# Differential attention in three steps per head, its factor on GpSimd, queries transposed two heads ahead

## The chip, the cores and the metric

The kernel runs on one core of a Trainium2 chip. A core has five engines with a queue each that is worked off in order: TensorE (PE in the profile, its weight loads as PEld), VectorE (DVE), ScalarE (ACT), GpSimd (POOL) and SyncE (SP), which issues DMAs. [...] The metric is the device time of one execution in microseconds (us), the median of several runs.

## The reference, cut to what matters

One transformer block on 512 tokens of width 1024, in fp32: two attention groups side by side on one projection, their joint output projection, a convolutional feed-forward net and a gated embedding. The change lies in the attention.

```
y_mla  = mla_group(...)                       # 8 heads, latent queries and keys
y_diff = diff_group(...)                      # 4 differential heads
x = x + concat([y_mla, y_diff]) @ w_out
x = x + conv_ffn(rms_norm(x), w_gate, w_up, conv_w, conv_b, w_down)
x = x + sigmoid(rms_norm(x) @ w_ple_gate) * (p @ w_ple_proj)

# diff_group, per head and block of queries: two maps m of 64 channels each
logits = einsum('bhqmd,bhmkd->bhmqk', qb, k_t) * scale + bias     # masked
probs  = softmax(logits)
attn   = probs[:, :, 0] - lam * probs[:, :, 1]
o      = rms_norm(attn @ v) * (1 - lam_init)
```

## The kernel before, in words

Every product in fp32 is made of three matmuls on a high and a low part (`mm3`, lines 157 to 159): high by high, low by high, high by low. Splitting a tile into the two parts takes an operation on ACT (high) and one on DVE (low).

The stages, by the span of the profiled execution: projections up to some 70 us; the latent heads (MLA), in 4 pairs by 4 tiles of 128 queries, from 70 to 151; the differential heads from 151 to 218; the rest of the output projection to 238; the feed-forward net to 600; the gated embedding to the end.

The differential stage runs 16 slots, 4 heads by 4 query tiles `t`, tile `t` seeing `(t + 1) * 128` keys. A slot `i` issues, in this order: the logits of slot `i + 2` (`diff_logits`: for each of the two maps the matmuls `dl` into a PSUM bank of the ring `lg`, of 3 banks; on DVE one pass that adds the bias strip and takes the maximum, L733, with a read of its accumulator; on ACT the exponential `pmd`, L734, which also sums the row into `s0` or `s1`); the combination of the two maps of slot `i + 2` (`diff_comb`: reciprocal of `s1` L742, factor `cf` L743, `pm0 + cf * pm1` L744, all on DVE); some units of filling work for PE (`pump`; a unit is six matmuls of 512 columns of the output projection, `o`, and every so often an addition to `x` on DVE, L682); the transposes `pTd` of slot `i`'s probabilities and their copy to SBUF on ACT; and the products `do` with the values for slot `i - 1`. Every head ends with a norm (`sqo`, `sso`, `mo`, `ro` as a power on GpSimd, `yd`) and the transposes `yT` of its output. `diff_T` transposes a head's queries (`d0T`) or keys (`d1T`) into the parts `st`. `FILL_DIFF` says how many units each slot takes; the 20 units come from the first four row blocks of `w_out` (16) and the next four (4). The high parts of the weights are cast on ACT (`hi_o`), the low ones are made on DVE (`lo_o`).

`probs_T` transposes and copies out at once; `mla_T` calls it for the latent heads. The order in which an engine meets its instructions is fixed when the program is built: it follows the order in which the code issues them, with some exchanged by the scheduler. The pool of `pm` tiles has 4 buffers, the PSUM ring `tp` of the transposes 2.

Of the kernel before, what the change touches and what calls it, by code (L numbers as in the profile page):

```python
# [59 lines left out]
FILL_UQ = (1, 1, 1, 1)  # L60
FILL_QK = 5
FILL_MLA = ((2, 2, 2, 2), (2, 2, 2, 2), (2, 2, 2, 2), (1, 1, 1, 1))
FILL_DIFF = ((2, 1, 1, 1), (1, 1, 2, 1), (1, 2, 2, 1), (1, 1, 2, 2))

UP_BANKS = ("lg", "tp", "tp", "ob")

# [28 lines left out]
def hybrid_block(ctx: ExitStack, tc: tile.TileContext, a: dict, out: bass.AP):  # L95
# [444 lines left out]
    pump(FILL_QK)  # L540


    def probs_T(pm, n, name, on_act):

        ps = bank("tp", f"pT{name}")
        for j in range(0, n, P):
            TE.transpose(ps[:, j:j + P], pm[:, j:j + P], ident)
        pt = pt_tile("pt")
        if on_act:
            S.copy(pt[:, :n], ps[:, :n])  # L550
        else:
            V.tensor_copy(pt[:, :n], ps[:, :n])
        return pt
# [62 lines left out]
    def mla_T(hp, t):  # L616

        n = (t + 1) * P
        pm, pmf, sums, one = mla.pop(("pm", hp, t))
        if one:  # L620
            pt = probs_T(pmf, 2 * n, f"m{hp}{t}", t)
            mla["pt", hp, t] = [pt[:, :n], pt[:, n:2 * n]]
        else:
            mla["pt", hp, t] = [probs_T(pm[c], n, f"m{hp}{t}{c}", c) for c in range(2)]

    def mla_pv(hp, t):

# [63 lines left out]
    def wo_units(kq, dqs, nk):  # L691

        for dq in dqs:
            w = wo_w(kq, dq)
            if kq == 0 and dq + 1 in dqs:
                with tc.issue_after(df["comb"].ins):
                    wo_first[0, dq + 1] = wo_w(0, dq + 1)
            if kq:
                wo2[dq] = w
            steps = [(b, k) for b in (2 * dq, 2 * dq + 1) for k in range(0, nk, 2)]  # L700
            if (kq, dq) == (0, 0):
                steps.sort(key=lambda s: s[1])
# [14 lines left out]
        split(h_, l_, ps, dcol if c == 0 else None)  # L717
        df["qk", h, c] = (h_, l_)

    def diff_logits(h, t):  # L720
        n = (t + 1) * P
        if t == 0:
            df["s0", h] = sm.tile([P, NT], F32, tag="s0", name="s0")
        s0 = df["s0", h][:, t:t + 1]
        (qh_, ql_), (kh_, kl_) = df["qk", h, 0], df["qk", h, 1]
        pms, s1 = [], sm.tile([P, 1], F32, tag="s1", bufs=4, name="s1")
        for m in range(2):
            r = slice(64 * m, 64 * m + 64)
            ps = bank("lg", f"dl{h}{t}{m}")
            mm3(ps[:, :n], [(qh_[r, tsl[t]], ql_[r, tsl[t]], kh_[r, :n], kl_[r, :n])])  # L730
            pm = pm_tile("pmd")
            nm = sm.tile([P, 1], F32, tag="nm", bufs=4, name="nmd")
            V.tensor_tensor_reduce(out=pm[:, :n], in0=ps[:, :n], in1=strips[0][:, h, T - n:], scale=1.0, scalar=3e38, op0=ALU.add, op1=ALU.min, accum_out=nm)  # L733
            S.activation(pm[:, :n], pm[:, :n], AF.Exp, bias=nm, scale=-1.0, accum_out=s0 if m == 0 else s1)  # L734
            pms.append(pm)
        df["pm", h, t] = pms, n, s0, s1

    def diff_comb(h, t):

        pms, n, s0, s1 = df["pm", h, t]  # L740
        cf = sm.tile([P, 1], F32, tag="cf", bufs=4, name="cf")
        V.reciprocal(cf, s1)  # L742
        V.scalar_tensor_tensor(cf, cf, nlam, s0, op0=ALU.mult, op1=ALU.mult)  # L743
        df["comb"] = V.scalar_tensor_tensor(pms[0][:, :n], pms[1][:, :n], cf, pms[0][:, :n], op0=ALU.mult, op1=ALU.add)  # L744
        df["pm", h, t] = pms[0]

    def diff_pv(h, t):
        if t == 0:
            df["po"] = bank("ob", f"do{h}")
        po, pt = df["po"], df.pop(("pt", h, t))  # L750
        for j in range(t + 1):
            TE.matmul(po[:, tsl[t]], pt[:, tsl[j]], zd[2][j][:, h * P:(h + 1) * P], start=j == 0, stop=j == t)
        if t < NT - 1:
# [7 lines left out]
        V.reduce_sum(sso, sq.rearrange("p (t d) -> p t d", d=P), axis=AX.X)
# [3 lines left out]
        V.scalar_tensor_tensor(mo, sso, 1.0 / P, mo, op0=ALU.mult, op1=ALU.add)  # L765
        G.tensor_tensor(ro, mo, mhalf[:, :NT], op=ALU.pow)
# [6 lines left out]
    dslots = [(h, t) for h in range(DH) for t in range(NT)]  # L773
    x_sb = []

    def load_x():
# [24 lines left out]
    def first_hi():
        raw = load_raw(a["w_out"][0, 0], 1024, "o00")
        w = [wts.tile([P, 1024], F32R, tag=i, bufs=NW, name=f"{i}_o00") for i in ("hi", "lo")]
        wo_first[0, 0] = w
# [8 lines left out]
        5: [zl(1), sq(0, 3), lambda: zd_root(0)],  # L813
        6: [sq(1, 0), zh(2)],
        7: [zl(2), zh(3)],
        8: [zl(3), sq(1, 1), zs(0, 0), first_hi],
        9: [zl(4), sq(1, 2)],
        10: [sq(1, 3), lambda: zd_root(1), zs(0, 1)],
        11: [zs(0, 2), zs(0, 3)],
        12: [load_x, zs(1, 0), zs(1, 1)],  # L820
        13: [zs(1, 2), zs(1, 3)],
    }
    late = {
        14: [yy(0)],
        15: [yy(1)],
    }
    mla_q(0)
    pump()
# [11 lines left out]
    for hp in range(HP):  # L840
        for t in range(NT):
            i = NT * hp + t
            last = hp == HP - 1
            n = FILL_MLA[hp][t]
            if t:
                mla_norm(hp, t)
            if t < NT - 1:
                mla_logits(hp, t + 1)
            if t == 2:
                for c, (d, m) in enumerate(((diff_T, (0, 0)), (diff_T, (0, 1))) if last else ((mla_q, (2 * hp + 2,)), (mla_k, (2 * hp + 2,)))):  # L850
                    d(*m)
# [717 lines left out]
```

## Time and profile before

| what | value |
|---|---|
| median of 3 runs | 644.52 us (644.42 to 644.86) |
| the profiled execution | 644.82 us, of which its span 643.0 us |
| PE busy | 632.4 us (98%) |
| DVE busy | 486.9 us (76%) |
| ACT busy | 360.2 us (56%) |
| POOL busy | 69.2 us (11%), 94 instructions |
| stage of the differential heads, 151 to 218 us | PE 64.65 of 67.0 us, DVE 56.0, ACT 43.0, POOL 3.0 |

The granted TensorE clock is full throughout. The profile gives the span of one execution on the slowest core; the time has 1.8 us more around it. An engine's busy time is the sum of its instructions' spans, and instructions of an engine overlap a little, so that the distance from one start to the next is what an instruction takes of the queue.

### The profile page before, as it was taken

What the parts mean: (1) busy time and instruction counts of PE and PEld (TensorE: products, weight loads), DVE (VectorE), ACT (ScalarE), POOL (GpSimd) and SP (SyncE); (2) the same over time, 40 slices, a digit from 0 to 9 for tenths busy, and PEclk for the clock granted to TensorE, in tenths of its full rate; (3) what the DMA queues carried; (4) which work ended last, traced back from release to release, by engine and by line L of the source; (5) the groups of instructions that cost most, each with busy time, mean ns of one, the idle gap of its engine ahead of it and who ended that gap; (6) DMA issues with size and microseconds to landing.
All of it is one profiled execution on the core that took longest, in us unless ns stands there. A gap on an engine that the chain in (4) does not pass through costs nothing.

```text
span 643.0 us, 10203 instructions
## 1 busy us (share of the span) xinstructions
PE 632.4 (98%) x3900; PEld 556.2 (87%) x3900; DVE 486.9 (76%) x870; ACT 360.2 (56%) x629; POOL 69.2 (11%) x94
## 2 busy tenths in 40 slices
PE   8999999999999999999999999999999999999997
PEld 8988888876777887889999999999999999988886
DVE  6889667887898678988876767676767777759844
ACT  7896567666667355557555545545454545637111
POOL 1514103030000130001000000000100000000000
PEclk9999999999999999999999999999999999999999
DMA  8241612330221437546865656464646554532021
GB/s 304 100 165 37 182 62 66 99 130 2 66 85 49 164 132 228 148 95 157 208 197 117 184 124 199 117 180 116 180 115 182 118 177 115 181 130 66 27 88 50
DMA packets 29912, 82.63 MB, mean 129 GB/s; under 512 B 3100, under 2 KB 4124, under 8 KB 29736
## 3 DMA queue, kind: packets, MB, share of 16 engines
q1 hardware_dynamic: 23816, 69.17, 32.3%
q0 software_dynamic: 5616, 12.33, 11.3%
q8 instruction: 31, 0.51, 0.3%
q10 hardware_dynamic: 432, 0.49, 0.2%
q14 instruction: 17, 0.14, 0.1%
HBM read 77.77 MB, written 5.52 MB: 130 GB/s over the span
## 4 chain that ended last, share of the span: by engine, by line
PE 86%; DVE 7%; ACT 3%; issue 2%; DMA 1%; ACTq 0%; DVEq 0%; SPq 0%
PE dn L157 6%; PE dn L158 6%; PE dn L159 6%; PE gx L159 4%; PE gx L158 4%; PE gx L157 4%; PE zd L157 3%; PE zd L159 3%; PE zd L158 3%; PE g L157 3%; PE g L158 3%; PE g L159 3%; PE pg L159 2%; PE pg L158 2%; PE pg L157 2%; PE o L157 2%
## 5 line engine op out<-in xcount | busy, mean ns | idle before, releaser
L954 DVE TENSOR_TENSOR wSl<-rS,wSh 128x1024 fp32r<-128x1024 f32 x21 | 25.7, 1224 | 43.4 <-ACT wSh L950 43.2
L157 PE MATMUL dn<-ah,hi_dn 128*128 128x512 f32 x144 | 56.2, 391 | 0.0
L158 PE MATMUL dn<-al,hi_dn 128*128 128x512 f32 x144 | 56.2, 391 | 0.0
L159 PE MATMUL dn<-ah,lo_dn 128*128 128x512 f32 x144 | 56.0, 389 | 0.0
L1071 POOL DMA_DIRECT2D rS<-in_w_gu x19 | 22.7, 1194 | 250.2 <-DVE cv L1239 129.9
L950 ACT CAST wSh<-rS 128x1024 fp32r<-128x1024 f32 x21 | 22.0, 1047 | 35.7 <-PE gy L158 35.4
L157 PE MATMUL zd<-hi_d,xh 128*128 128x512 f32 x96 | 39.1, 407 | 0.0
L158 PE MATMUL zd<-lo_d,xh 128*128 128x512 f32 x96 | 37.6, 392 | 0.0
L682 DVE TENSOR_TENSOR x<-x,dn 128x512 f32<-128x512 f32 x44 | 29.9, 679 | 6.1 <-PE dn L159 6.1
L954 DVE TENSOR_TENSOR wTl<-rA,wTh 128x1024 fp32r<-128x1024 f32 x19 | 23.3, 1225 | 13.7 <-ACT wTh L950 13.2
L159 PEld LDWEIGHTS dn<-ah,lo_dn 128*128 128x128 f32 x144 | 27.0, 188 | 5.8
L157 PEld LDWEIGHTS dn<-ah,hi_dn 128*128 128x128 f32 x144 | 27.1, 188 | 5.1
L158 PEld LDWEIGHTS dn<-al,hi_dn 128*128 128x128 f32 x144 | 27.1, 188 | 5.0
L954 DVE TENSOR_TENSOR wAl<-rA,wAh 128x1024 fp32r<-128x1024 f32 x21 | 25.6, 1217 | 2.7 <-ACT wAh L950 2.7
L950 ACT CAST wAh<-rA 128x1024 fp32r<-128x1024 f32 x21 | 22.1, 1050 | 9.7 <-DMA rA<-in_w_gu 9.5
L1242 ACT ACTIVATE cv<-cv 128x512 f32<-128x512 f32 x22 | 13.9, 630 | 23.9 <-DVE cv L1239 23.8
L157 PE MATMUL g<-b2h,wAh 128*128 128x256 f32 (+1 forms) x88 | 26.4, 300 | 0.5 <-ACT g L1195 0.5
L157 PE MATMUL o<-yh,hi_o 128*128 128x512 f32 x64 | 26.8, 419 | 0.0
L734 ACT ACTIVATE pmd<-pmd,nmd 128x128 f32<-128x128 f32 (+3 forms) x32 | 17.9, 560 | 15.1 <-DVE nmd L733 15.0
L159 PE MATMUL g<-b2h,wAl 128*128 128x256 f32 (+1 forms) x88 | 26.2, 297 | 0.0
L158 PE MATMUL g<-b2l,wAh 128*128 128x256 f32 (+1 forms) x88 | 26.2, 297 | 0.0
L1462 ACT ACTIVATE sg<-sg 128x512 f32<-128x512 f32 (+1 forms) x9 | 5.3, 584 | 36.8 <-DVE sg L1461 36.8
(475 smaller groups left out, 2219.1 us busy)
## 6 DMA issues: line engine op xcount, KB each, us to landing
rA<-in_w_gu SPq DMA_DIRECT2D x22, 512.0 KB, 3.7
rS<-in_w_gu SPq DMA_DIRECT2D x22, 512.0 KB, 3.7
rS<-in_w_gu POOLq DMA_DIRECT2D x19, 512.0 KB, 6.1
raw_dn<-in_w_down SPq DMA_DIRECT2D x18, 512.0 KB, 5.9
raw_d<-in_w_d SPq DMA_DIRECT2D x12, 512.0 KB, 3.4
r<-in_w_gu SPq DMA_DIRECT2D x19, 256.0 KB, 5.9
raw_o<-in_w_out SPq DMA_DIRECT2D x8, 512.0 KB, 3.6
rS_pg<-in_w_pg SPq DMA_DIRECT2D x6, 512.0 KB, 4.1
```

The costliest lines, as they stand in the source:

```text
L157: TE.matmul(ps, xh, wh, start=first and i == 0, stop=False, skip_group_check=again)
L158: TE.matmul(ps, xh, wl, start=False, stop=False, skip_group_check=again)
L159: TE.matmul(ps, xl, wh, start=False, stop=last and i == n - 1, skip_group_check=again)
L682: V.tensor_tensor(xb(b), xb(b), ps, op=ALU.add)
L734: S.activation(pm[:, :n], pm[:, :n], AF.Exp, bias=nm, scale=-1.0, accum_out=s0 if m == 0 else s1)
L950: S.copy(h_, src)
L954: V.tensor_tensor(l_, src, _f32(h_), op=ALU.subtract)
L1071: nc.gpsimd.dma_start(sums[f].rearrange("p (i c) -> p i c", i=2), a["w_gu"][f][:, :2048].rearrange("p (i c) -> p i c", i=2)[:, :, :512], a ...
L1242: S.activation(cv, cv, AF.Silu)
L1462: S.activation(sg, sg, AF.Sigmoid)
```

## The change

Five things are altered together:

- The head's four query tiles are worked in three steps (`GROUPS`): tiles 0 and 2 together, with 128 and 384 keys side by side in one PSUM bank for each map; then tile 1 (256 keys); then tile 3 (512). There are 12 slots in place of 16. The matmuls, maxima, exponentials and combinations are the same in number and size; the copies of transposed probabilities are 12 in place of 16.
- The factor `cf` is computed by three GpSimd instructions of one column each (power -1 against a tile of minus ones, times `nlam`, times `s0`), in place of two on DVE.
- The queries of head `h + 2` are transposed in the middle slot of head `h`; before, those of head `h + 1` in the first slot of head `h`. Head 1's are transposed ahead of the loop.
- `probs_T` is parted: `probs_T` transposes, `probs_out` copies. In the latent heads the last tile of a pair (`t == 3`) issues the maxima and exponentials of the next pair's first tile between the two.
- The units of filling work are dealt out anew, 5 for heads 0 to 2 each and 4 for head 3; two loads of `w_out` are split earlier; the low part of one latent output (`yh1`) is made later.

```diff
-FILL_DIFF = ((2, 1, 1, 1), (1, 1, 2, 1), (1, 2, 2, 1), (1, 1, 2, 2))
+FILL_DIFF = ((2, 1, 2), (2, 1, 2), (2, 1, 2), (1, 1, 2))
...
+    GROUPS = ((0, 2), (1,), (3,))
+    def diff_logits(h, g):
+        ts = GROUPS[g]
...
+        for t in ts:
+            at[t] = slice(n, n + (t + 1) * P)
+            n += (t + 1) * P
+        pms, pss = [], [bank("lg", f"dl{h}{g}{m}") for m in range(2)]
+        for t in ts:
+            for m, ps in enumerate(pss):
+                r = slice(64 * m, 64 * m + 64)
+                mm3(ps[:, at[t]], [(qh_[r, tsl[t]], ql_[r, tsl[t]], kh_[r, :(t + 1) * P], kl_[r, :(t + 1) * P])])
+        for m, ps in enumerate(pss):
             pm = pm_tile("pmd")
-            V.tensor_tensor_reduce(out=pm[:, :n], in0=ps[:, :n], ...)
-            S.activation(pm[:, :n], pm[:, :n], AF.Exp, bias=nm, scale=-1.0, accum_out=s0 if m == 0 else s1)
+            for i, t in enumerate(ts):
+                c = at[t]
+                V.tensor_tensor_reduce(out=pm[:, c], in0=ps[:, c], ...)
+                S.activation(pm[:, c], pm[:, c], AF.Exp, bias=nm, scale=-1.0, accum_out=s0[:, t:t + 1] if m == 0 else s1[:, i:i + 1])
...
-        V.reciprocal(cf, s1)
-        V.scalar_tensor_tensor(cf, cf, nlam, s0, op0=ALU.mult, op1=ALU.mult)
-        df["comb"] = V.scalar_tensor_tensor(pms[0][:, :n], pms[1][:, :n], cf, pms[0][:, :n], op0=ALU.mult, op1=ALU.add)
+        for i, t in enumerate(GROUPS[g]):
+            c, cf = at[t], sm.tile([P, 1], F32, tag="cf", bufs=4, name="cf")
+            G.tensor_tensor(cf, s1[:, i:i + 1], mone, op=ALU.pow)
+            G.tensor_tensor(cf, cf, nlam, op=ALU.mult)
+            G.tensor_tensor(cf, cf, df["s0", h][:, t:t + 1], op=ALU.mult)
+            df["comb"] = V.scalar_tensor_tensor(pms[0][:, c], pms[1][:, c], cf, pms[0][:, c], op0=ALU.mult, op1=ALU.add)
...
             mla_T(hp, t)
-            z_flush()
+            if t < 3:
+                mla_pt(hp, t)
+                z_flush()
             if i:
                 mla_pv(*divmod(i - 1, NT))
-            if t == 3 and not last:
-                mla_logits(hp + 1, 0)
-                for c in range(2):
-                    mla_exp(hp + 1, 0, c)
+            if t == 3:
+                if not last:
+                    mla_logits(hp + 1, 0)
+                    for c in range(2):
+                        mla_exp(hp + 1, 0, c)
+                mla_pt(hp, t)
+                z_flush()
...
-        if h + 1 < DH and t == 0:
-            diff_T(h + 1, 0)
+        if g == 1 and h + 2 < DH:
+            diff_T(h + 2, 0)
-        if t == 3 and h + 2 < DH:
+        if g == 2 and h + 2 < DH:
             diff_T(h + 2, 1)
```

What this does to the queues is seen at three places; `[waits ...]` names the engines on whose semaphores a row waits. First DVE at the end of head 1. `ISA` is the pass over the logits and the read of its accumulator, `SCALAR_TENSOR_TENSOR pmd<-pmd,cf` the combination. Before:

```order
L733 ISA pmd,nmd<-dl_2119,strip 128x512 [waits DVE_49,PE_49]
L733 ISA nmd 128x1
L765 SCALAR_TENSOR_TENSOR mo<-sso,mo 128x4 [waits DVE_49]
L189 SCALAR_TENSOR_TENSOR st<-d0T_2103,dcol,st 128x512 [waits Activation_49]
L682 TENSOR_TENSOR x_1643<-x_1643,o_2077 128x512 [waits PE_49]
L742 RECIPROCAL cf<-s_2110 128x1 [waits Activation_49]
L769 TENSOR_TENSOR yd_2092<-yd_2092,ro 128x512 [waits Pool_49]
L743 SCALAR_TENSOR_TENSOR cf<-cf,nlam,s_1968 128x1 [waits DVE_49]
```

and now:

```order
L756 ISA pmd,nmd<-dl_2082,strip 128x512 [waits PE_49]
L756 ISA nmd 128x1
L795 SCALAR_TENSOR_TENSOR mo<-s_1958 128x4 [waits Activation_49]
L769 SCALAR_TENSOR_TENSOR pmd<-pmd,cf 128x512 [waits Activation_49,Pool_49]
L696 TENSOR_TENSOR x_1645<-x_1645,o_2102 128x512 [waits PE_49]
L792 TENSOR_REDUCE sso<-sqo 128x4 [waits Activation_49]
L796 SCALAR_TENSOR_TENSOR mo<-sso,mo 128x4 [waits DVE_49]
L800 TENSOR_TENSOR yd_2127<-yd_2127,ro 128x512 [waits Activation_49,Pool_49]
L756 ISA pmd,nmd<-dl_2140,strip 128x128 [waits PE_49]
```

The rows between the last pass over the logits and the combination are fewer, the combination waits on GpSimd, `yd` stands right behind the `mo` whose power GpSimd takes, and the next slot's passes stand behind all of it.

The second place is the queue of GpSimd in this stage. Before, it holds the four powers `ro` of the heads' norms:

```order
L165 TENSOR_TENSOR rd<-rs_m,mhalf 128x32 [waits DVE_49] x2
L766 TENSOR_TENSOR ro<-mo,mhalf 128x4 [waits DVE_49] x2
L766 TENSOR_TENSOR ro<-mo,mhalf 128x4 [waits DVE_49,Pool_49] x2
L1007 TENSOR_TENSOR nr_2678<-nr_2678,nsq 128x512 [waits PE_49,Activation_49]
L1007 TENSOR_TENSOR nr_2678<-nr_2678,nsq 128x512 [waits Activation_49,Pool_49] x2
```

and now, at the end of head 1 and the start of head 2, with three rows for each factor:

```order
L766 TENSOR_TENSOR cf<-s_2080,mone 128x1 [waits Activation_49]
L767 TENSOR_TENSOR cf<-cf,nlam 128x1 [waits Pool_49]
L768 TENSOR_TENSOR cf<-cf,s_1958 128x1 [waits Pool_49]
L797 TENSOR_TENSOR ro<-mo,mhalf 128x4 [waits DVE_49]
L766 TENSOR_TENSOR cf<-s_2139,mone 128x1 [waits Activation_49]
L767 TENSOR_TENSOR cf<-cf,nlam 128x1 [waits Pool_49]
L768 TENSOR_TENSOR cf<-cf,s_2138 128x1 [waits Pool_49]
```

Each row of a factor waits for the one before it.

The third is PE ahead of the logits of head 2's tile of 256 keys. Before:

```order
L547 MATMUL pTd_2188<-ident,pmd 128x128 [waits PE_49]
L547 MATMUL pTd_2188<-ident,pmd 128x128 x2
L752 MATMUL do_2143<-zd_1470,pt 128x128 [waits Activation_49]
L752 MATMUL do_2143<-zd_1477,pt 128x128
L665 MATMUL yT_2196<-ident,yd_2092 128x128 [waits DVE_49,PE_49]
L665 MATMUL yT_2196<-ident,yd_2092 128x128 x3
L157 MATMUL dl_2206<-st 128x256
L158 MATMUL dl_2206<-st 128x256
L159 MATMUL dl_2206<-st 128x256
L157 MATMUL dl_2214<-st 128x256 [waits DVE_49]
```

and now:

```order
L783 MATMUL do_2196<-zd_1479,pt 128x128
L783 MATMUL do_2196<-zd_1757,pt 128x128
L729 MATMUL d0T_2201<-ident,zd_791 128x128
L729 MATMUL d0T_2201<-ident,zd_799 128x128
L729 MATMUL d0T_2201<-ident,zd_807 128x128
L729 MATMUL d0T_2201<-ident,zd_815 128x128
L157 MATMUL dl_2210<-st 128x256 [waits DVE_49]
L158 MATMUL dl_2210<-st 128x256
L159 MATMUL dl_2210<-st 128x256
L157 MATMUL dl_2211<-st 128x256 [waits DVE_49]
```

Both banks are now waited for on DVE's semaphore; the bank that `dl_2211` takes is the one that the pass over the 384 logits of the slot before reads.

More of the change, by code (lines that the diff above doesn't have):

```diff
@@ L197, in hybrid_block @@
     V.memset(mhalf, -0.5)
+    mone = small("mone", [P, 1])
+    V.memset(mone, -1.0)
     S.activation(warm[:, :1], ones[:, :1], AF.Exp)
@@ L540, in hybrid_block, with probs_T @@
     pump(FILL_QK)
-    def probs_T(pm, n, name, on_act):
+    def probs_T(pm, n, name):
         ps = bank("tp", f"pT{name}")
@@ L547, in probs_T, with probs_out @@
             TE.transpose(ps[:, j:j + P], pm[:, j:j + P], ident)
+        return ps
+    def probs_out(ps, n, on_act):
         pt = pt_tile("pt")
@@ L620, in mla_T, with mla_pt @@
         if one:
-            pt = probs_T(pmf, 2 * n, f"m{hp}{t}", t)
+            mla["pT", hp, t] = [probs_T(pmf, 2 * n, f"m{hp}{t}")]
+        else:
+            mla["pT", hp, t] = [probs_T(pm[c], n, f"m{hp}{t}{c}") for c in range(2)]
+    def mla_pt(hp, t):
+        n, ps = (t + 1) * P, mla.pop(("pT", hp, t))
+        if t < 2:
+            pt = probs_out(ps[0], 2 * n, t)
             mla["pt", hp, t] = [pt[:, :n], pt[:, n:2 * n]]
         else:
-            mla["pt", hp, t] = [probs_T(pm[c], n, f"m{hp}{t}{c}", c) for c in range(2)]
+            mla["pt", hp, t] = [probs_out(ps[c], n, c) for c in range(2)]
     def mla_pv(hp, t):
@@ L694, in wo_units @@
             w = wo_w(kq, dq)
-            if kq == 0 and dq + 1 in dqs:
+            if kq == 0 and 0 < dq and dq + 1 in dqs:
                 with tc.issue_after(df["comb"].ins):
@@ L718, in diff_T @@
         df["qk", h, c] = (h_, l_)
-    def diff_logits(h, t):
-        n = (t + 1) * P
-        if t == 0:
+    GROUPS = ((0, 2), (1,), (3,))
+    def diff_logits(h, g):
+        ts = GROUPS[g]
+        if g == 0:
             df["s0", h] = sm.tile([P, NT], F32, tag="s0", name="s0")
-        s0 = df["s0", h][:, t:t + 1]
+        s0, s1 = df["s0", h], sm.tile([P, 2], F32, tag="s1", bufs=4, name="s1")
         (qh_, ql_), (kh_, kl_) = df["qk", h, 0], df["qk", h, 1]
[L726 to L730, printed above, removed]
-            pm = pm_tile("pmd")
-            nm = sm.tile([P, 1], F32, tag="nm", bufs=4, name="nmd")
-            V.tensor_tensor_reduce(out=pm[:, :n], in0=ps[:, :n], in1=strips[0][:, h, T - n:], scale=1.0, scalar=3e38, op0=ALU.add, op1=ALU.min, accum_out=nm)
-            S.activation(pm[:, :n], pm[:, :n], AF.Exp, bias=nm, scale=-1.0, accum_out=s0 if m == 0 else s1)
-            pms.append(pm)
-        df["pm", h, t] = pms, n, s0, s1
@@ L738, in diff_comb @@
[L738 to L748, printed above, removed]
-            df["po"] = bank("ob", f"do{h}")
[L750 to L753, printed above, removed]
+        at, n = {}, 0
@@ new lines, in diff_logits @@
+        for t in ts:
[7 more added lines that the diff above has]
+        for m, ps in enumerate(pss):
+            pm = pm_tile("pmd")
+            for i, t in enumerate(ts):
+                c = at[t]
+                nm = sm.tile([P, 1], F32, tag="nm", bufs=4, name="nmd")
+                V.tensor_tensor_reduce(out=pm[:, c], in0=ps[:, c], in1=strips[0][:, h, T - (t + 1) * P:], scale=1.0, scalar=3e38, op0=ALU.add, op1=ALU.min, accum_out=nm)
+                S.activation(pm[:, c], pm[:, c], AF.Exp, bias=nm, scale=-1.0, accum_out=s0[:, t:t + 1] if m == 0 else s1[:, i:i + 1])
+            pms.append(pm)
@@ new lines, in diff_logits, with diff_comb @@
+        df["pm", h, g] = pms, n, at, s1
+    def diff_comb(h, g):
+        pms, n, at, s1 = df["pm", h, g]
+        for i, t in enumerate(GROUPS[g]):
[4 more added lines that the diff above has]
+            df["comb"] = V.scalar_tensor_tensor(pms[0][:, c], pms[1][:, c], cf, pms[0][:, c], op0=ALU.mult, op1=ALU.add)
+        df["pm", h, g] = pms[0], n, at
@@ new lines, in diff_probs, with diff_pv @@
+    def diff_probs(h, g):
+        pm, n, at = df.pop(("pm", h, g))
+        df["pt", h, g] = probs_out(probs_T(pm, n, f"d{h}{g}"), n, True), at
+    def diff_pv(h, g):
+        if g == 0:
+            df["po"] = bank("ob", f"do{h}")
+        po, (pt, at) = df["po"], df.pop(("pt", h, g))
+        for t in GROUPS[g]:
+            for j in range(t + 1):
+                c = at[t].start + j * P
+                TE.matmul(po[:, tsl[t]], pt[:, c:c + P], zd[2][j][:, h * P:(h + 1) * P], start=j == 0, stop=j == t)
+        if g < 2:
@@ L771, in diff_pv @@
             df["scale"] = df["scaling"]()
-    dslots = [(h, t) for h in range(DH) for t in range(NT)]
+    dslots = [(h, g) for h in range(DH) for g in range(3)]
     x_sb = []
@@ L799, in hybrid_block, with first_hi @@
     z2_lo = lambda kq: lo(*z2_[kq])
[L801 to L804, printed above, removed]
+    def first_hi(dq):
+        raw = load_raw(a["w_out"][0, dq], 1024, f"o0{dq}")
+        w = [wts.tile([P, 1024], F32R, tag=i, bufs=NW, name=f"{i}_o0{dq}") for i in ("hi", "lo")]
+        wo_first[0, dq] = w
         z2_.append((*hi(raw, w[0]), w[1]))
@@ L815, in hybrid_block @@
         7: [zl(2), zh(3)],
-        8: [zl(3), sq(1, 1), zs(0, 0), first_hi],
+        8: [zl(3), sq(1, 1), zs(0, 0), lambda: first_hi(0)],
         9: [zl(4), sq(1, 2)],
@@ L819, in hybrid_block @@
         11: [zs(0, 2), zs(0, 3)],
-        12: [load_x, zs(1, 0), zs(1, 1)],
+        12: [load_x, zs(1, 0), zs(1, 1), lambda: first_hi(1)],
         13: [zs(1, 2), zs(1, 3)],
@@ L824, in hybrid_block @@
         14: [yy(0)],
-        15: [yy(1)],
     }
@@ L882, in hybrid_block @@
     mla_pv(HP - 1, NT - 1)
+    y_hl(1, ymn[1])
+    diff_comb(0, 0)
     y_hl(3, mla["po"])
-    diff_comb(0, 0)
     diff_T(1, 1)
     y_hl(2, ymn[2])
+    diff_T(1, 0)
     diff_comb(0, 1)
+    z2_lo(5)
     region.__exit__(None, None, None)
     pump()
-    for i, (h, t) in enumerate(dslots):
+    for i, (h, g) in enumerate(dslots):
         if i + 2 < len(dslots):
@@ L893, in hybrid_block @@
             diff_comb(*dslots[i + 2])
-        pump(FILL_DIFF[h][t])
-        df["pt", h, t] = probs_T(df.pop(("pm", h, t)), (t + 1) * P, f"d{h}{t}", True)
+        pump(FILL_DIFF[h][g])
+        diff_probs(h, g)
         if i:
             diff_pv(*dslots[i - 1])
-        if h + 1 < DH and t == 0:
-            diff_T(h + 1, 0)
-        if h and t == 1:
+        if g == 1 and h + 2 < DH:
+            diff_T(h + 2, 0)
+        if h and g == 1:
             df["scaling"]()
-        if t == 3 and h + 2 < DH:
+        if g == 2 and h + 2 < DH:
             diff_T(h + 2, 1)
-        if h and t == 2:
+        if h and g == 2:
             y_split(4 + h - 1, df["y", h - 1], ocol, "tp")
-        if h and t == 3:
-            if h == 2:
-                fill.append(wo_units(1, range(2), 2))
+        if h == 2 and g == 2:
+            fill.append(wo_units(1, range(2), 2))
     pump()
```

## The prediction

> **What bounds the kernel now.** I read the windows of the differential stage first, then what PE waited for in it, then the groups by line and form for prices, and the timeline for what one start has from the next. The sum of five windows from 151 to 218 us:
>
> ```profile
> sum 67.00, PE 64.65 PEld 51.12 DVE 56.01 ACT 43.03 POOL 3.02; mean PE 12.93 PEld 10.22 DVE 11.20 ACT 8.61 POOL 0.60
> ```
>
> PE has 2.35 us free in 67 and DVE 11, so PE bounds the stage and DVE is not far. PE's waits between 130 and 240 us, longest first:
>
> ```profile
> PE dl L159 <- DVE st L189: 0.9, 2, 0.6
> PE mo L633 <- DVE pt L552: 0.7, 1, 0.7
> PE pTd L547 <- ACT pt L550: 0.5, 1, 0.5
> ```
>
> All that can be gained from waits is 2.1 us. DVE's free time is not spare either, as its timeline around one factor shows:
>
> ```profile
> 176.58 0.17 DVE L742 RECIPROCAL cf<-s 128x1 f32<-128x1 f32 x1 [0.90 <-ACT pmd L734]
> 176.78 0.22 DVE L743 SCALAR_TENSOR_TENSOR cf<-cf,nlam,s 128x1 f32<-128x1 f32 x1
> 177.03 0.62 DVE L744 SCALAR_TENSOR_TENSOR pmd<-pmd,cf 128x384 f32<-128x384 f32 x1
> 177.57 0.68 DVE L733 CUSTOM_DVE_ANT_0 pmd<-dl,strip 128x512 f32<-128x512 f32 x1
> 178.18 0.08 DVE L733 DVE_READ_ACCUMULATOR2_ANT nmd<- 128x1 f32 x1
> 178.18 0.68 DVE L761 TENSOR_REDUCE sso<-sqo 128x4 f32<-128x512 f32 x1
> 178.78 0.68 DVE L733 CUSTOM_DVE_ANT_0 pmd<-dl,strip 128x512 f32<-128x512 f32 x1
> ```
>
> DVE stands 0.90 us for the exponential, then spends 0.45 on the factor; the next pass over logits, which frees a bank for PE, stands behind both. From start to start an instruction takes 0.06 to 0.08 less than its span. The prices, DVE and ACT:
>
> ```profile
> L151 DVE TENSOR_TENSOR lo_o<-raw_o,hi_o 128x1024 fp32r<-128x1024 f32 x7 | 8.5, 1217 | 0.0
> L682 DVE TENSOR_TENSOR x<-x,o 128x512 f32<-128x512 f32 x12 | 8.1, 682 | 0.1
> L733 DVE CUSTOM_DVE_ANT_0 pmd<-dl,strip 128x512 f32<-128x512 f32 x8 | 5.4, 679 | 0.0
> L733 DVE CUSTOM_DVE_ANT_0 pmd<-dl,strip 128x384 f32<-128x384 f32 x8 | 4.3, 550 | 0.3 <-PE dl L159 0.2
> L743 DVE SCALAR_TENSOR_TENSOR cf<-cf,nlam,s 128x1 f32<-128x1 f32 x16 | 3.5, 218 | 0.4
> L733 DVE CUSTOM_DVE_ANT_0 pmd<-dl,strip 128x256 f32<-128x256 f32 x8 | 3.3, 418 | 0.0
> L744 DVE SCALAR_TENSOR_TENSOR pmd<-pmd,cf 128x512 f32<-128x512 f32 x4 | 3.0, 750 | 0.1
> ...
> L742 DVE RECIPROCAL cf<-s 128x1 f32<-128x1 f32 x16 | 2.6, 160 | 3.8 <-ACT pmd L734 3.7
> L744 DVE SCALAR_TENSOR_TENSOR pmd<-pmd,cf 128x384 f32<-128x384 f32 x4 | 2.5, 615 | 0.1
> L189 DVE SCALAR_TENSOR_TENSOR st<-d0T,dcol,st 128x512 fp32r<-128x512 f32 x3 | 2.2, 746 | 0.1
> L733 DVE CUSTOM_DVE_ANT_0 pmd<-dl,strip 128x128 f32<-128x128 f32 x8 | 2.2, 288 | 0.9 <-PE dl L159 0.6
> ```
>
> ```profile
> L734 ACT ACTIVATION_READ_ACCUMULATOR pmd<-pmd,nmd 128x1 f32 x32 | 6.0, 189 | 0.0
> L734 ACT ACTIVATE pmd<-pmd,nmd 128x512 f32<-128x512 f32 x8 | 5.8, 724 | 2.3 <-DVE nmd L733 2.3
> L734 ACT ACTIVATE pmd<-pmd,nmd 128x384 f32<-128x384 f32 x8 | 4.9, 613 | 4.2 <-DVE nmd L733 4.1
> L150 ACT CAST hi_o<-raw_o 128x1024 fp32r<-128x1024 f32 x4 | 4.2, 1050 | 2.2 <-DMA raw_o<-in_w_out 2.1
> ```
>
> Combinations and exponentials of 256 and 128 keys, whose rows I leave out, follow the same step from 512 to 384: 0.48 and 0.50 for 256. And PE:
>
> ```profile
> 172.93 0.50 PE L157 MATMUL o<-yh,hi_o 128*128 128x512 f32 x1
> ...
> 174.42 0.27 PE L547 MATMUL pTd<-ident,pmd 128*128 128x128 f32 x1
> 174.53 1.06 PE L752 MATMUL do<-zd,pt 128*128 128x128 f32 x8
> 175.42 0.60 PE L715 MATMUL d0T<-ident,zd 128*128 128x128 f32 x4
> 175.95 0.50 PE L157 MATMUL dl<-st 64*128 64x512 f32 x2
> ```
>
> A unit right after `dl` takes 1.49 (172.93 to 174.42), a transpose 0.11, four blocks of `do` 0.89. Four transposes should take 0.44 and took 0.53: some 0.09 are lost on going over to `dl`, and I take as much for the way back (1.49 against the 1.4 that I count for a unit elsewhere).
>
> **The change, part by part.**
>
> Three steps. The same matmuls in 12 slots: four changes to `dl` and back fewer, 4 x 0.18 = 0.7, with fewer units right behind `dl` 0.9 in all. ACT has four copies fewer, off the path.
>
> Fill without an empty slot: the wait of `pTd` (0.5) lay at the slot for which no unit was left. All have one now: 0.5 gone.
>
> Last slot before the stage: `mo` waited 0.7 for DVE's copy. The copy on ACT stands behind four exponentials of the new first step now; I leave 0.45, and the second `dl` bank behind it waits 0.35 for the pass over 384: together nothing gained.
>
> Queries two heads ahead: the 0.9 for `st` goes. With the above PE alone is 0.9 + 0.5 + 0.9 = 2.3 us shorter.
>
> Maxima ahead of the P copies: at three boundaries of latent head pairs two exponentials (ACT) and two reductions (DVE) come ahead of the copies that the next products need. Two units of fill lie between, some 2.8 us against under 1 us: nothing; without that cover 3 x 0.9. The second load of `w_out` cast earlier lies in the latent stage with the same cover: nothing.
>
> The factor. DVE loses 16 pairs, 16 x (0.16 + 0.22) = 6.0 by spans, some 5.6 from start to start. GpSimd gets 48 instructions. The nearest rows:
>
> ```profile
> L766 POOL TENSOR_TENSOR ro<-mo,mhalf 128x4 f32<-128x4 f32 x4 | 4.0, 1006 | 79.7 <-DVE mo L765 79.7
> ...
> L165 POOL TENSOR_TENSOR rl<-rs_m,mhalf 128x8 f32<-128x8 f32 x1 | 1.7, 1652 | 0.8 <-DVE rs_m L164 0.8
> ```
>
> ```profile
> 26.07 0.22 POOL L383 TENSOR_TENSOR krt<-za,rs_k 128x16 f32<-128x16 f32 x1
> 26.37 0.35 POOL L384 TENSOR_TENSOR kr<-kr,krt 128x32 f32<-128x32 f32 x1
> ...
> 27.13 0.40 POOL L383 TENSOR_TENSOR krt<-za,rs_k 128x16 f32<-128x16 f32 x1
> ```
>
> A power takes 0.16 per column, so one column 1.01 - 3 x 0.16 = 0.53. A dependent product starts 0.30 after the start of the one before it. With a hop in (I take 0.15) a factor is 0.15 + 0.53 + 0.08 + 0.30 + 0.22 + 0.03 = 1.3 us after the exponential, in place of 0.45; a second one of the same step comes 1.15 later. Bounds: products that cost only their hops, 0.85; products half way to the slow one shown (0.40), each 0.15 slower, 1.6. I take 1.3, nearest to the dependent pair shown.
>
> [...]
>
> What is queued behind: the combination now stands right behind its step's last pass, so DVE waits for exponential and factor with little else to do, and the next passes, which free PE's score banks, stand behind it. With three banks and two per slot, the second bank of a slot needs the first pass (in step 0 the 384 one) of the slot before. Walking down both queues, from the first tile of head 1:
>
> - Head 1, step 0 to step 1. PE: unit 1.4, pTd 0.2, do 0.9, d0T 0.4, dl 0.75: 3.7. DVE from the end of that `dl`: pass 0.55, comb 512 0.67, passes 0.84, x 0.6, then the first factor (a `hi_o` cast of 1.05 stands between the exponentials on ACT) and the second 1.15 after it, combs 0.8: 5.7. DVE 2.0 late.
> - Step 1 to step 2. PE: two units, pTd, do, d1T, dl: 5.1. DVE: pass, st, pass 1.5; exponential with its read 0.7 and factor 1.3; comb 0.4, lo_o 1.13, x 0.6, st 0.67: 6.3. Late 3.2.
> - Step 2 to the second bank of head 2's step 1. PE: two units, pTd, do, dl, unit, pTd, do, d0T: 8.5. DVE: passes 1.36, exponential and factor 2.1, comb 0.67, x and sso 1.2, mo 0.1, ro on GpSimd 0.15 + 1.01, yd 0.6, passes 0.84: 8.1. PE waits 2.8.
> - Then by the same counting 1.1 at head 2's step 2 (two factors and a lo_o ahead of the pass), 2.0 at the transposes after it (their bank waits for the keys' `st`, behind lo_o, lo_o and a factor), 1.2 at head 3's step 1.
>
> That makes 7.1. My PE pieces are some 2 us short of PE's busy time of the stage (they add to 60.0 from first `dl` to last product where the windows leave 62), time in which DVE catches up: 5.1 to 5.2. The tail has enough cover.
>
> Sum: 5.2 - 2.3 = 2.9 us longer. The profiled execution (644.82, span 643.0) is 0.3 above the median 644.52; a difference carries over, so 647.4. Some 6.5 factors lie on this chain, so each 0.1 us in a factor moves the time 0.65: 644.5 at 0.85, 649.4 at 1.6.
>
> **The rivals.**
>
> - Faster: a factor comes in the 0.5 us that DVE needed, or DVE finds other work while it waits. All waits of the walk go and 2.3 us are gained: 642.2. For it speaks that DVE sheds 5.6 us in a stage where PE waited for it; against it the power's row alone. It decides below 0.85 us a factor.
> - Same: the factor is near 0.85, the products nearly free; gain and wait cancel: 644.5. Against it the 0.30 between dependent products.
> - Much slower: GpSimd's small operations are drawn out while DVE reads two operands. The same form took 0.22 once and 0.40 another time; 0.2 more on each product is 0.4 x 6.5 = 2.6 more: 650.0. [...]
>
> **How the numbers follow.** A measurement of this kernel tells a change of 0.2%, 1.3 us, from none. The forecast (645.9 to 649.4) has 0.58, for its prices are rows and only the products' size is not; much slower 0.06; same 0.12; faster 0.24, since a walk by hand can miss that lateness is made up. Slower 0.64, same 0.12, faster 0.24. The forecast's own range is 645.9 to 649.4; for 8 in 10 it reaches down into the faster case, to 642.8, and up to 649.4.
>
> **What would show it.** Right: PE waits for DVE of 2 to 3 us at head 2's step 1 and at about 1 to 2 us at three places behind; DVE idle ahead of most combinations, released by POOL, 10 us or more in the stage; a factor of 1.3 us on GpSimd by starts; the 0.9 and 0.5 of before gone; PE busy in the stage about 0.9 less. Wrong: combinations that wait under 0.5 us for POOL, or PE without waits although they do; or a wait in the latent stage at the pairs' boundaries.

## The result, and the profile after

| kernel | median | range | runs |
|---|---|---|---|
| before | 644.69 us | 644.42 to 645.25 | 4 |
| changed | 653.16 us | 652.07 to 654.42 | 4 |

The changed kernel is slower: ratio 1.013, 95% interval 1.0116 to 1.0144, 8.5 us. The forecast was 647.4 us, with a range from 645.9 to 649.4: the direction was right, but the time lies 3.8 us above the range.

The changed kernel's profiled execution took 652.07 us (span 650.3 against 643.0). Its differential stage, by windows (from, to, length, then busy time of PE, PEld, DVE, ACT and POOL, granted clock, DMA share, GB/s):

```profile
151.00:162.00 11.00, 10.76 (x85) 7.81 (x84) 7.83 (x23) 7.17 (x20) 3.12 (x9) 1.00 0.00 1
162.00:175.00 13.00, 13.00 (x81) 10.30 (x80) 8.63 (x26) 8.17 (x22) 3.62 (x12) 1.00 0.11 42
175.00:188.00 13.00, 10.81 (x67) 8.68 (x66) 8.22 (x22) 6.68 (x18) 2.85 (x8) 1.00 0.11 42
188.00:203.00 15.00, 12.40 (x64) 9.34 (x63) 12.24 (x23) 8.91 (x18) 3.80 (x10) 0.77 0.39 116
203.00:218.00 15.00, 13.63 (x81) 10.60 (x80) 9.86 (x29) 8.74 (x25) 5.19 (x13) 1.00 0.07 26
sum 67.00, PE 60.60 PEld 46.72 DVE 46.78 ACT 39.67 POOL 18.58; mean PE 12.12 PEld 9.34 DVE 9.36 ACT 7.93 POOL 3.72
```

GpSimd is busy 18.6 us in place of 3.0, and PE idles 6.4 of 67 us in place of 2.35. DVE is busy 46.8 us in place of 56.0, but the changed stage is not over at 218 us: from its first `dl` to its last `do` DVE is busy 49.9 us in place of 55.1, which is 5.2 less. In the fourth row the granted clock has fallen to 0.77; taken in shorter windows it is 0.50 from 192.7 to 199.5 us, for 6.8 us, and 1.00 in the rest of the stage. What PE waited for between 150 and 226 us (total, times, longest wait):

```profile
PE o L158 <- DVE yh5l L189: 1.4, 1, 1.4
PE d1T L729 <- DVE st L189: 1.3, 1, 1.3
PE yT L679 <- ACT pt L556: 1.3, 1, 1.3
PE dl L157 <- DVE nmd L756: 1.2, 1, 1.2
PE do L783 <- ACT yd L790: 1.0, 1, 1.0
PE o L158 <- DVE yh6l L189: 0.3, 1, 0.3
PE mo L647 <- DVE pt L558: 0.2, 1, 0.2
```

That is 6.4 us up to the last product of the stage, where before had 2.1. DVE for its part, in the same stretch:

```profile
DVE pmd L769 <- POOL cf L768: 15.3, 13, 2.0
DVE yd L800 <- POOL ro L797: 1.7, 2, 1.1
```

One factor, followed over three engines in the timeline (start, duration, engine):

```profile
173.06 0.51 ACT L757 ACTIVATE pmd<-pmd,nmd 128x256 f32<-128x256 f32 x1 [0.48 <-DVE nmd L756]
173.47 0.18 ACT L757 ACTIVATION_READ_ACCUMULATOR pmd<-pmd,nmd 128x1 f32 x1
...
173.74 0.54 POOL L766 TENSOR_TENSOR cf<-s,mone 128x1 f32<-128x1 f32 x1 [2.79 <-ACT pmd L757]
...
174.35 0.19 POOL L767 TENSOR_TENSOR cf<-cf,nlam 128x1 f32<-128x1 f32 x1
174.62 0.19 POOL L768 TENSOR_TENSOR cf<-cf,s 128x1 f32<-128x1 f32 x1
174.84 0.49 DVE L769 SCALAR_TENSOR_TENSOR pmd<-pmd,cf 128x256 f32<-128x256 f32 x1 [1.90 <-POOL cf L768]
```

The row's sum is read at 173.65, the combination starts at 174.84: 1.19 us, where the prediction had 1.3. DVE stood 1.90 us, exponential included.

And PE where the clock fell:

```profile
189.62 0.61 PE L783 MATMUL do<-zd,pt 128*128 128x128 f32 x4
191.55 0.66 PE L729 MATMUL d1T<-ident,zd 128*128 128x128 f32 x4 [1.32 <-DVE st L189]
193.48 1.12 PE L679 MATMUL yT<-ident,yd 128*128 128x128 f32 x4 [1.28 <-ACT pt L556]
...
197.13 0.63 PE L159 MATMUL o<-yh,lo_o 128*128 128x512 f32 x1
197.56 0.63 PE L157 MATMUL o<-yh,hi_o 128*128 128x512 f32 x1
...
199.61 0.39 PE L159 MATMUL o<-yh,lo_o 128*128 128x512 f32 x1
```

The clock falls during the second of two waits within 4 us, and behind it a matmul of 512 columns starts every 0.43 us in place of 0.23, up to about 199 us. Stage by starts, from the first `dl` to the end of the last `do`: 151.73 to 224.07, 72.3 us; before 151.76 to 217.15, 65.4. So 6.9 of the 7.3 us of span lie in the stage: 4.3 more of listed waits and, by the fourth experiment below, some 2.6 of clock. The other 0.4 lies right behind it, where `o` waits for `yh6l`, which no `o` did before. The saving of PE's own 0.9 us is not seen in this sum; one reason is that at least one wait cost more than is listed: from `do` at 189.62, four records of 0.11, to `d1T` at 191.55 are 1.49 us, 0.17 more than the 1.32 of the row.

The clock's part is that of this one execution. The mean granted clock was 0.994 to 0.995 in three of the four runs of the changed kernel and 1.000 in the fourth, which took 653.12 us and was no faster than the others.

### The profile page after: what moved, and what is told of

Same layout as the page of the kernel before. It is cut to its first block, busy times and chain, and to the rows that moved or that the text cites. A ratio compares the mean times of both kernels' runs of the same rounds, so it can differ in the third digit from the quotient of the medians.

```text
span 650.3 us, 10214 instructions
## 1 busy us (share of the span) xinstructions
PE 635.7 (98%) x3900; PEld 558.3 (86%) x3900; DVE 481.4 (74%) x839; ACT 358.2 (55%) x625; POOL 85.2 (13%) x142
## 4 chain that ended last, share of the span: by engine, by line
PE 83%; DVE 7%; ACT 4%; issue 2%; POOL 2%; DMA 1%; ACTq 0%; DVEq 0%
PE dn L158 6%; PE dn L157 6%; PE dn L159 6%; PE gx L159 4%; PE gx L158 4%; PE gx L157 4%; PE zd L157 3%; PE zd L159 3%; PE zd L158 3%; PE g L157 3%; PE g L158 3%; PE g L159 3%; PE pg L157 2%; PE pg L158 2%; PE pg L159 2%
## 5 line engine op out<-in xcount | busy, mean ns | idle before, releaser
L611 ACT ACTIVATE pm<-ml,sums,rq 128x128 f32<-128x128 f32 (+3 forms) x32 | 19.6, 616 | 16.3 <-DVE sums L597 10.8
```

Source lines behind the costliest of these rows:

```text
L611: S.activation(pm[c], ps[c], AF.Exp, bias=nm[:, c:c + 1], scale=r[:, c:c + 1], accum_out=sums[:, 1, c:c + 1])
```

## The experiments

Theory A: the factor's way over GpSimd holds DVE's in-order queue, PE waits behind it and its clock falls. Rival B: the three steps and the new places of the transposes cost the time. All runs were timed against the kernel before, which was 644.3 to 644.6 in each set. An edit to the source can also exchange neighbours in an engine's queue, since the order is fixed anew for each build; run 14 says where that bears on the reading.

**1. Factor on DVE.**

```diff
-            G.tensor_tensor(cf, s1[:, i:i + 1], mone, op=ALU.pow)
-            G.tensor_tensor(cf, cf, nlam, op=ALU.mult)
-            G.tensor_tensor(cf, cf, df["s0", h][:, t:t + 1], op=ALU.mult)
+            V.reciprocal(cf, s1[:, i:i + 1])
+            V.scalar_tensor_tensor(cf, cf, nlam, df["s0", h][:, t:t + 1], op0=ALU.mult, op1=ALU.mult)
```

> The changed kernel with the factor back on DVE (reciprocal and one product) and all else as changed. Theory A (the factor's way over GpSimd holds DVE's queue, PE waits, and its clock then falls): PE's waits in the differential stage fall from 6.5 us to under 2, the granted clock stays full, and the time is 642 to 644. Theory B (three steps and the new places of the transposes are what hurts, the factor little): the time stays over 650, with waits of yT, d1T and the score bank.

Measured: 647.25 us, 1.0039 of before (1.0026 to 1.0053). 5.9 us come back, but 2.7 stay: A has the larger part and not all. The clock stayed full, as A said, but PE's listed waits in the stage are 3.1 us and not under 2, and the range given for A was missed.

**2. The old 16 steps, factor on GpSimd.** The same three instructions put into the kernel before.

> The kernel before, its 16 steps and places, with the factor alone on GpSimd (three instructions). A: slower than before by 3 us or more, since DVE waits some 1.2 us longer at each of 16 combinations; with more combinations apart it can be worse than the changed kernel. B: within 1 us of before.

Measured: 655.99 us, ratio 1.0176 (1.0163 to 1.0189). The factor alone costs 11.4 us with 16 steps. DVE waited 19.0 us for it, and PE's listed waits in the stage are 7.5 us, `o` 2.5 and `d0T` 1.6 the largest. B is not needed for a loss of this size.

**3. Combination later, factor on GpSimd.**

```diff
+        if i + 1 < len(dslots):
+            diff_comb(*dslots[i + 1])
         if i + 2 < len(dslots):
             diff_logits(*dslots[i + 2])
-            diff_comb(*dslots[i + 2])
```

> The changed kernel with each combination issued at the start of the next slot in place of right behind its own logits, so that some other work (weights' low parts, additions) comes ahead of it on DVE; GpSimd does the same. A: DVE's waits for GpSimd fall from 15 us to 8 to 11, PE's waits to 2 to 4, the clock stays full: 645 to 648. B: no change, 651 to 654.

Measured: 649.96 us, ratio 1.0078 (1.0066 to 1.0091): 3.2 us less with the same work on GpSimd, though above the 645 to 648 of A. DVE's waits for GpSimd hardly fell (14.8 us), against what I expected, and PE's listed waits in the stage were 6.4 us, as many as in the changed kernel; but the clock stayed at 1.00 in every window of the stage. So the two profiles differ by the clock and not by the waits. That the 3.2 us of the medians are the clock's is not shown: the changed kernel's run at a full clock took 653.12 us.

**4. PE kept busy in the gaps.** Products of head 1's second step repeated three times ahead of `d1T` and three times ahead of `yT`.

```diff
+        if (h, g) == (1, 1):
+            again(h, g, pt, at, 3)
...
             diff_T(h + 2, 1)
+            if h == 1:
+                df["again"]()
```

> The changed kernel with twelve products of head 1's second step repeated (2.6 us of matmuls, same result) in the two gaps ahead of d1T and yT at 190 to 193.5 us, where PE waits anyway. A with the clock as a term of its own: the granted clock stays 1.0 behind the gaps, some 3 us that were lost at half clock come back, 649 to 651. If the clock has nothing to do with the idle time: same clock loss, 653 to 655.

Measured: 654.62 us, ratio 1.0156 (1.0142 to 1.0171): no time won at the end, inside the range of the second branch, but for another reason. In the windows the clock holds where it fell before:

```profile
194.00:199.00 5.00, 4.69 (x26) 3.35 (x25) 4.08 (x6) 2.12 (x3) 0.72 (x3) 1.00 0.62 166
199.00:203.00 4.00, 3.75 (x28) 2.83 (x27) 1.91 (x6) 2.71 (x6) 0.17 (x1) 1.00 0.49 195
203.00:210.00 7.00, 3.87 (x17) 3.28 (x18) 5.53 (x15) 5.52 (x14) 3.18 (x8) 0.76 0.00 0
```

From `yT` (193.52) to the end of the two units behind it, PE took 4.5 us (to 198.02, where it waits 0.31 for the transposes' bank); the changed kernel took 7.06 for the same work (193.48 to 200.54). These 2.6 us are the clock's. They were lost again at 206 us, where `do` waits for a copy on ACT:

```profile
206.13 1.92 PE L791 MATMUL do<-zd,pt 128*128 128x128 f32 x8 [3.39 <-ACT yd L801]
```

ACT's copy `yd` stood behind the cast of the gated embedding's input `pT`, which had waited 3.53 us for its DMA and began at 200.29 us; in the changed kernel the same cast began at 200.32, so it did not come earlier with PE. After these 3.4 us the clock fell to 0.50 for 3.4 us, 0.76 in the mean of the last row. The local price of the clock is shown; that the whole time falls by it is not.

**5. One GpSimd instruction per factor, 11. five.** The power alone on GpSimd with the products on DVE; and two more products by -1.

```diff
# 5
-            G.tensor_tensor(cf, cf, nlam, op=ALU.mult)
-            G.tensor_tensor(cf, cf, df["s0", h][:, t:t + 1], op=ALU.mult)
+            V.scalar_tensor_tensor(cf, cf, nlam, df["s0", h][:, t:t + 1], op0=ALU.mult, op1=ALU.mult)
# 11
+            G.tensor_tensor(cf, cf, mone, op=ALU.mult)
+            G.tensor_tensor(cf, cf, mone, op=ALU.mult)
```

> The changed kernel with one GpSimd instruction per factor (the power) and the two products in one DVE instruction: a dose between the factor on DVE (647.3) and three instructions on GpSimd (653.2). A (the wait grows with the factor's way): a factor of some 0.9 us, DVE's waits for GpSimd of 8 to 11 us, time 648 to 651.5. B (any trip over GpSimd costs the same, as soon as PE's clock falls): 652 to 654.

> The changed kernel with two more GpSimd products by -1 in each factor (same result): a factor of some 1.9 us in place of 1.3. By the walk's slope, 0.65 us per 0.1 us of factor, 3.5 us slower than changed: 656 to 658. If PE's waits have their own limit or the clock loses no more: 653.5 to 655.5.

Measured: 648.51 us (1.0064, 1.0052 to 1.0076) and 658.1 (1.0212, 1.0195 to 1.0229). With none, one, three and five instructions on GpSimd the time is 647.3, 648.5, 653.2 and 658.1: it grows with the length of the way. Run 5 lies in the range of A, with 7.1 us of DVE's waits for GpSimd (8 to 11 expected); run 11 lies 0.1 us above its first range. A dependent product takes 0.27 from start to start (174.35, 174.62), so five are 0.54 longer than three and cost 4.9 us, 0.9 per 0.1 us where the walk had 0.65. The clock stayed full with one and fell with three and five (0.77 in the stretch from 188 to 203 us with five). With five it was at 0.50 for 10.2 us of the stage and the part behind it, with three for 6.8, so the 0.9 is not all waits.

**6 and 7. Transposes spread over the steps**, queries in step 0, keys in step 1, with the factor on DVE and on GpSimd.

```diff
-        if g == 1 and h + 2 < DH:
+        if g == 0 and h + 2 < DH:
             diff_T(h + 2, 0)
-        if g == 2 and h + 2 < DH:
+        if g == 1 and h + 2 < DH:
             diff_T(h + 2, 1)
```

> Factor on DVE as in the run before that, and the transposes of the head after next spread over the steps: queries in step 0, keys in step 1, the output's in step 2, in place of queries in step 1 and keys and output both in step 2. C (the remaining loss is the two transpose banks: d1T waits for the query split on DVE, yT for the copy on ACT): the waits of d1T 1.6 and yT 1.3 go, 644 to 645.5. D (the remaining loss is DVE's order at large): they come back under another name, 646.5 to 648.

> The same spread transposes with the factor on GpSimd as changed. A: still well over before, 649 to 652, since the score banks wait for DVE; C alone (transposes are the main cost, GpSimd only lengthens their wait): under 647.

Measured: 649.67 us (1.0077, 1.0065 to 1.0089) and 653.36 (1.0141, 1.0127 to 1.0154). On DVE it is 2.4 us worse than the places of the change and above both ranges: C falls, and D gave too little. `d1T` now waits 1.8 us in one piece, and `o` 2.0 for the high and low parts of `yh`. With the factor on GpSimd the time is above both ranges too, and the new places change nothing (653.36 against 653.16).

**8. Latent heads as before, factor on DVE.** The copies of P back ahead of the next maxima.

> Factor on DVE, three steps, and in the latent heads the copies of P back ahead of the next pair's maxima, as before the change. If the maxima ahead are worth something, it is slower than the 647.3 of the factor on DVE by up to 1 us; if they cost, faster by up to 1; I expect no difference (within 1 us): PE's waits in the latent stage are 0.8 us in both.

Measured: 647.02 us (1.0035, 1.0021 to 1.005) against 647.25: no difference, as the prediction had it, as far as runs that spread over 3 us can tell.

**9. Combination later, factor on DVE; 13. the same in the old 16 steps.**

> Three steps with the factor on DVE and each combination issued at the start of the next slot. With the factor on GpSimd this place gave back 3.2 us (653.2 to 650.0). If what is left of the loss (2.7 us over before) is DVE standing for the exponentials ahead of its own queue, it falls from 647.3 to 644 to 646; if it is the three steps themselves (four passes and four exponentials in a row, two transposes in one step), it stays at 647 to 648.

> The kernel before (16 steps, factor on DVE) with each combination issued at the start of the next slot. If the place of the combination is worth the same with any number of steps, it gains up to the 0.9 us of waits for DVE: 643.3 to 644.3. If it only undoes what the three steps had put in a row, nothing: 644.2 to 645.2.

Measured: 644.67 us (1.0006, 0.9997 to 1.0015) and 645.42 (1.0016, 1.0007 to 1.0024). With three steps the place is worth 2.6 us, with 16 it costs 1.0, a little above both ranges. So the place is worth nothing by itself; it mends something that came with the rest of the change. In the profile that is the wait of `d1T`, 1.6 us in run 1 and none in run 9.

**10. The old 16 steps with the queries two heads ahead.**

```diff
-        if h + 1 < DH and t == 0:
-            diff_T(h + 1, 0)
+        if t == 1 and h + 2 < DH:
+            diff_T(h + 2, 0)
```

> The kernel before with one part of the change alone: the queries of the head after next transposed in the second slot, head 1's ahead of the loop. The prediction counts 0.9 us for the waits for st that this takes away. If the gain is real apart from the three steps: 643.2 to 644.2. If the three steps are not what costs the rest but the moved transposes are: 645.5 or more.

Measured: 645.16 us, ratio 1.0017 (1.0006 to 1.0027). The waits for `st` (0.9 us before) are gone, and in their place stand

```profile
PE pTd L547 <- ACT pt L550: 1.3, 1, 1.3
PE mo L633 <- DVE pt L552: 0.8, 1, 0.8
PE d1T L715 <- DVE yh4l L189: 0.7, 1, 0.7
```

where `pTd` had 0.5 and `d1T` nothing. The time lies between the two ranges, 0.8 us above before. In the old 16 steps the gain that the prediction booked for this part does not exist; in three steps it was not tried by itself.

**12. As 9, with head 0's output transposes a slot later.**

> Three steps, factor on DVE, combinations at the start of the next slot (644.7), and the output transposes of head 0 one slot later, out of the slot that transposes keys too. If the 1.2 us that yT waited there for a copy on ACT is PE's last large wait, it goes and the time is 643 to 644. If the wait moves on (two transpose banks, DVE full), 644.2 to 645.5.

Measured: 644.7 us (1.0001, 0.9992 to 1.001). The wait of `yT`, 1.2 us, is gone from the profile, and the time is the same, as the second branch said.

**14. One cast moved, factor on DVE; 16. the same with the factor on GpSimd.** In run 1 ACT had, ahead of the last two exponentials of head 1's first step,

```profile
170.54 1.05 ACT L150 CAST hi_o<-raw_o 128x1024 fp32r<-128x1024 f32 x1 [1.35 <-DMA raw_o<-in_w_out]
...
171.50 0.40 ACT L755 ACTIVATE pmd<-pmd,nmd 128x128 f32<-128x128 f32 x1
...
172.02 0.17 DVE L764 RECIPROCAL cf<-s 128x1 f32<-128x1 f32 x1 [1.33 <-ACT pmd L755]
...
173.72 0.75 DVE L189 SCALAR_TENSOR_TENSOR st<-d0T,dcol,st 128x512 fp32r<-128x512 f32 x1
...
174.61 0.63 PE L727 MATMUL d1T<-ident,zd 128*128 128x128 f32 x4 [1.34 <-DVE st L189]
```

a weight's cast that waited for its DMA; behind it the exponential, the reciprocal, the query split, and PE. The weight is first used at 207.5 us, by `o`. The cast was tied behind the step's exponentials:

```diff
+            if kq and dq == 0:
+                with tc.issue_after(df["exp"].ins):    # last exponential of head 1, step 0
+                    w = wo_w(kq, dq)
```

> Three steps with the factor on DVE (647.3) and one instruction moved: the cast of a weight on ACT, which in that run waited 1.35 us for its DMA at 170.5 us ahead of two exponentials of head 1's first step, is ordered behind those exponentials. If the wait of d1T for the query split (1.34 us at 174.6) came from this cast through exponential, reciprocal and combination, it goes, and the time is 645.4 to 646.4. If DVE's queue would have been as late without the cast: 646.8 to 647.8.

> The changed kernel, factor on GpSimd, with the same cast moved behind the exponentials. There the cast did not wait for its DMA, so if GpSimd's factor alone holds DVE: 651.5 to 653.5. If the cast is the cause of the loss with any factor: under 650.5.

Measured: 644.7 us (1.0003, 0.9994 to 1.0012) and 652.81 (1.0124, 1.0108 to 1.014). On DVE this edit was worth 2.5 us, nearly all that was left and more than the first branch gave it: the profile after the move has PE waits of 1.3 (`yT`), 0.3 and 0.2, and no wait of `d1T`. With GpSimd it changes nothing. Between these two, the factor alone is 8.1 us.

More than the cast moved, though. In run 14's queues the query split's ACT half, at 168.29 us, stands ahead of the two exponentials and its DVE half, at 169.81 us, ahead of the two combinations; in run 1 both stand behind. So the 2.5 us belong to this order as a whole. The cast's wait is probably most of it: the combinations of run 14 end at 171.81, so a split behind them, 0.67 long, would end by some 172.5 at the latest, by this estimate 0.2 after the 172.30 at which `d1T` starts there, where run 1 had a wait of 1.34. No run moves the cast alone.

**15. All three moves, factor on DVE.**

> Three steps, factor on DVE, with all three moves together: the weight's cast behind the exponentials, each combination at the start of the next slot, head 0's output transposes one slot later. Each alone brought 644.7. If what each leaves is a different wait, their sum is under before: 643.2 to 644.1. If the floor is PE's own work and the stage's ends, 644.3 to 645.

Measured: 645.06 us (1.001, 0.9999 to 1.0021). PE's listed waits in the stage are down to 1.0 us, and the time is that of before, at the upper end of the second range. No version beat the kernel before.

## Why the prediction missed, step by step

**The mechanism was right.** DVE stands ahead of most combinations, released by GpSimd, 15.3 us (said: 10 or more); the factor takes 1.19 us where it was followed (said: 1.3); PE waits for DVE in the middle of the stage. The 0.15 us for the hop into GpSimd was my estimate, and no run shows it: in the changed kernel a power starts 0.07 to 0.09 us after ACT's read ends wherever GpSimd stood free. That the factor on GpSimd is the main cause is shown by three pairs of runs whose sources differ in it alone: 11.4 us in 16 steps (run 2), 5.9 as changed (run 1) and 8.1 with the cast moved (runs 14 and 16). The price depends on what else stands in the queues.

**The step that failed is "Sum: 5.2 - 2.3".** By runs 14 and 16 the 5.2 of the factor is 8.1, and the 2.3 of gain is nothing (run 14 equals before). The first half was nearly right as waits: 6.4 us listed in the changed kernel for 5.2 that remained after the walk. They lie at other places, though: 2.2 us around head 2's step 1 (said 2.8), nearly half of it by ACT's `yd`; 2.6 at the transposes of step 2 (said 2.0, at `pTd`, by the keys' split); nothing at head 2's step 2 and head 3's step 1 (said 1.1 and 1.2), but 1.4 at head 3's first unit of the second weights, whose `yh5l` came late. What failed is the booked gain, and the price of a wait.

**The gain of 2.3 was booked and is not there.** The walk took before's waits (0.9 and 0.5) off because their named causes went. Run 10 shows in the old steps that the 0.9 comes back as 1.3 (0.5 before) and 0.7 at the next places. With no GpSimd at all the changed kernel is 2.7 us slower than before, and not 2.3 faster as my rival "faster" had it; 2.5 of that went with one edit, which moved a cast on ACT from ahead of two exponentials and the query split with it (run 14). The prediction saw this cast, "a `hi_o` cast of 1.05 stands between the exponentials on ACT", but priced it only in the step with GpSimd's factor. Of the 0.9 of PE's own work little is seen. From first `dl` to last `do`, less the listed waits, PE takes 63.3 us before (65.4 - 2.1), 62.1 in run 9 (64.0, from 152.77 to 216.80, - 1.9), 62.8 in run 14 and 63.2 in runs 1 and 15. In each of these four `o` also waits 0.3 us for `yh6l` right behind the stage, which it did not before. No median fell by it.

**PE's clock had no term.** I priced a wait at its own length. In the profiled execution the clock was also at half for 6.8 us from the second of two waits of 1.3 us, 2.6 us more by run 4; the run at a full clock, no faster, has no trace. The slow stretches, at 0.50, lasted 3.4 us (runs 2, 4 and 8) or twice that, 6.8 (changed, and run 7). The length of a single wait does not account for the fall: in the changed kernel none was over 1.4 us; in run 8 the clock fell right behind one of 1.9 us, while one of 1.8 in run 6 and two of 1.7 and 0.8 close together in run 3 left it full. What exactly tips it is open.

**What the parts were worth.** Maxima ahead of the P copies: nothing (run 8, as said). All parts but the factor together: nothing that is measurable, in the order of run 14; the three steps by themselves were not tried. Queries two heads ahead, in the old steps: 0.8 us of loss (run 10, said 0.9 of gain). The factor on GpSimd: 5.9 to 11.4 us of loss (said 5.2).

**The rivals.** "Same" and "faster" asked for a factor under 0.85 us; runs 1 and 5 are nearest to that and both slower than before, and run 14 only equals it. "Much slower" was nearest in size (650.0), and what it named was seen in part. Of GpSimd's 32 products 31 took 0.19 us and one 0.59, while DVE made `yh1l`; and three of the 16 powers were drawn out, to 1.27, 0.88 and 1.08 us beside 0.54 elsewhere, each while DVE ran a `TENSOR_TENSOR` on two tiles in SBUF (`lo_o` twice, `yd` once). The first:

```profile
192.69 1.22 DVE L151 TENSOR_TENSOR lo_o<-raw_o,hi_o 128x1024 fp32r<-128x1024 f32 x1
...
193.03 1.27 POOL L766 TENSOR_TENSOR cf<-s,mone 128x1 f32<-128x1 f32 x1 [4.00 <-ACT pmd L757]
```

Each of the three ends 0.39 to 0.40 us after DVE's instruction; powers beside DVE's combinations or additions to `x` took 0.54 or 0.55. The three powers are 1.6 us longer together. How much of it reached PE is not shown.

**Left open.** The changed kernel's profiled run is the fastest of its four; the others are 1 to 2.4 us slower, and only this one has a trace. Where the remaining time of those goes, that of the run at a full clock above all, is not known.

## What to carry to other kernels

An instruction moved off a busy engine costs that engine the round trip, if what needs the result stands next in its queue: count the way there and back (1.19 us against 0.45 here) times the places where nothing else stands between, and not the engine's busy time, which fell by 5.2 us in this stage while the kernel lost 8.5. Waits of the matmul engine can cost twice, as in one profiled execution here: 6.4 us as waits and, by run 4, some 2.6 as clock. When a reordering loses, look for a foreign instruction that waits for a DMA ahead of the chain: here an edit that moved one weight's cast in ACT's queue, and the query split with it, was worth 2.5 us, and the weight was needed 37 us later. A wait whose cause is gone is not yet a gain: look for the next wait behind it.

## What the runs showed of the hardware that I had not expected

One wait cost PE 0.17 us more than the idle time listed (1.49 for 1.32). The half clock (0.50) came in stretches of 3.4 us (run 4) or 6.8 (changed). Three GpSimd powers that ran beside a DVE `TENSOR_TENSOR` on two SBUF tiles ended 0.39 to 0.40 us after it and took 0.88 to 1.27 us in the changed kernel. Its GpSimd products of one column took 0.19 us in 31 of 32 cases, with 0.27 from one dependent start to the next where it was followed, and the other 13 powers of one column took 0.54 or 0.55, as the line through the wider ones said (0.53).
